# A branch hint at the head of ScalarE's and VectorE's streams, for a taken branch at their end

## The chip, the cores and the metric

The kernel runs on one core of one Trainium2 chip. The metric is device time in microseconds; the time before is the median of four runs, 162.29 us (162.15 to 162.35). The profile is of one further execution, with its own time.

## The reference

```python
def setup_inputs():
    batch, seq, dim = 32, 512, 1024
    return {"x": np.random.randn(batch, seq, dim).astype(np.float32)}

def reference(x):
    relu_x = np.maximum(x, 0)
    return np.mean(relu_x, axis=-1).astype(np.float32)
```

Each of the 16,384 rows of 1,024 float32 numbers is clipped at zero and averaged. The input has 64 MiB, the output 64 KiB.

## The kernel before, in words

The rows are laid over the 128 partitions so that each partition holds 128 neighbouring rows (`J` = 128). A tile is 16 of them for every partition (`NB` = 16): 128 x 16 x 1024 numbers, 8 MiB. There are seven full tiles (`full` = 7) in three buffers, `rows0` to `rows2` (`BUFS` = 3). The eighth tile comes in smaller and smaller pieces so that little work is left behind the last byte: `row_pieces` of 8, 4, 2 and 1 rows, and the last row as `col_pieces` of 512, 256 and 256 columns, in a tile of its own, `last`. All loads and the store are issued by SP, in this order, on one queue. Each load has a semaphore of its own, `loaded[i]`, which counts to 16 when all sixteen transfer engines have landed their share. From the fourth tile on SP waits (`buf_free`) until ScalarE and VectorE have finished the tile that held the buffer.

ScalarE takes the even rows (`act_row`, L15: an activation with Relu and a sum into one column of `sums`), VectorE the odd ones (`dve_row`, L20: a maximum with zero and a sum). In the trace each such row is two instructions, the operation and the read of its accumulator. Both write their elementwise result back over the input. GpSimd scales finished columns of `sums` into `res` (L132, L155). The second-last row is split between ScalarE (448 columns) and VectorE (576). Of the last row, ScalarE takes the first 512 columns, VectorE the next 256, and then VectorE, at L165, takes the last 256 columns and two extra columns in which the partial sums of the other two pieces stand. So L165 ends the last mean. SP waits for it, stores `res` (L173), clears the semaphores (L177) and waits for the store (L178).

The order on every engine is that in which the function writes it: there is no scheduler. The frame around the kernel has three barriers of all engines at the start, one at L195 and two at L55; `issue_ahead_of_entry_barrier` moves the first load on SP ahead of the first of them. A branch from the frame's first block to the kernel's block (L206) stands on every engine between the first barrier and the second. ScalarE's first instruction behind the barriers is a load of its function table, and GpSimd's is the fill of `scale`, which VectorE waits for before its first row.

The program consists of one stream of instructions for each engine. ScalarE's and VectorE's streams are the long ones, with 131 and 132 recorded instructions that count as work; the loops over rows are written out, so neither stream has a loop.

Of the kernel before, what the change touches and what calls it, by code (L numbers as in the profile page):

```python
# [1 line left out]

# [4 lines left out]

F32 = mybir.dt.float32
ALU = mybir.AluOpType
ACT = mybir.ActivationFunctionType  # L10


def act_row(nc, src, acc):

    return nc.scalar.activation(out=src, in_=src, func=ACT.Relu, accum_out=acc)  # L15


def dve_row(nc, src, acc, init=None):

    return nc.vector.tensor_scalar(  # L20
        out=src, in0=src, scalar1=0.0, scalar2=init,
        op0=ALU.max, op1=ALU.add, accum_out=acc,
    )


def issue_ahead_of_entry_barrier(nc):


    entry, body = nc.cur_f.blocks[0].instructions, None
    for block in nc.cur_f.blocks[1:]:  # L30
        for k, ins in enumerate(block.instructions):
            if ins.opcode == "DMACopy":
                body, load = block.instructions, k
                break
        if body is not None:
            break
    first = body[load]
    assert first.engine == mybir.EngineType.SP and not first.sync_info.on_wait
    assert all(i.opcode in ("Drain", "EventSemaphore") or i.engine != first.engine for i in body[:load])
    del body[load]  # L40
    at = next(k for k, i in enumerate(entry) if i.engine == first.engine and i.opcode == "Drain")
    entry.insert(at, first)


@with_exitstack
def kernel(
    ctx: ExitStack,
    tc: tile.TileContext,
    x: bass.AP,
    out: bass.AP,  # L50
):


    tc.close()
    tc.compile()  # L55

    nc = tc.nc
    P = nc.NUM_PARTITIONS
    xf = x.flatten_outer_dims()
    R, D = xf.shape  # L60
    assert R % P == 0
    J = R // P
    inv = 1.0 / D
    xr = xf.rearrange("(p j) d -> p j d", p=P, j=J)
    outr = out.flatten().rearrange("(p j) -> p j", p=P, j=J)

    NB = 16
    BUFS = 3
    full = J // NB - 1

    row_pieces = [8, 4, 2, 1]
    assert sum(row_pieces) == NB - 1
    col_pieces = [512, 256, 256]
    assert sum(col_pieces) == D

    def sbuf(name, *shape):
        return ctx.enter_context(nc.sbuf_tensor(name, list(shape), F32))

    bufs = [sbuf(f"rows{b}", P, NB, D) for b in range(BUFS)]
    sums, res, part = sbuf("sums", P, J), sbuf("res", P, J), sbuf("part", P, 2)  # L80


    last = sbuf("last", P, D + 2)
    scale = sbuf("scale", P, D // 4 + 2)


    loaded = [nc.alloc_semaphore(f"loaded{i}") for i in range(full + len(row_pieces) + len(col_pieces))]
    act, dve, pool = (nc.alloc_semaphore(n) for n in ("act", "dve", "pool"))
    stored = nc.alloc_semaphore("stored")


    def load(i, dst, src):
        nc.sync.dma_start(out=dst, in_=src).then_inc(loaded[i], 16)

    def buf_free(t):

        if t >= BUFS:
            nc.sync.wait_ge(act, t - BUFS + 1)
            nc.sync.wait_ge(dve, t - BUFS + 1)

    for t in range(full):
        buf_free(t)
        load(t, bufs[t % BUFS][:, :, :], xr[:, t * NB:(t + 1) * NB, :])
    j0 = full * NB
    buf_free(full)
    xt = bufs[full % BUFS]
    lo, i = 0, full
    for n in row_pieces:
        load(i, xt[:, lo:lo + n, :], xr[:, j0 + lo:j0 + lo + n, :])
        lo, i = lo + n, i + 1  # L110
    c = 0
    for w in col_pieces:
        load(i, last[:, c:c + w], xr[:, J - 1, c:c + w])
        c, i = c + w, i + 1


    nc.gpsimd.memset(scale[:, :], inv).then_inc(pool, 1)  # L117

    def rows(i, xt, lo, n, j0):
        nc.scalar.wait_ge(loaded[i], 16)  # L120
        nc.vector.wait_ge(loaded[i], 16)
        for k in range(lo, lo + n):
            j = j0 + k
            done = (dve_row if j % 2 else act_row)(nc, xt[:, k, :], sums[:, j:j + 1])
            if k >= lo + n - 2:
                done.then_inc(dve if j % 2 else act, 1)

    def finish(after, lo, hi):

        nc.gpsimd.wait_ge(act, after)  # L130
        nc.gpsimd.wait_ge(dve, after)
        nc.gpsimd.tensor_scalar(  # L132
            out=res[:, lo:hi], in0=sums[:, lo:hi], scalar1=inv, scalar2=0.0, op0=ALU.mult, op1=ALU.add,
        )

    nc.vector.wait_ge(pool, 1)
    for t in range(full):
        rows(t, bufs[t % BUFS], 0, NB, t * NB)
    finish(full, 0, j0)
    lo, i = 0, full  # L140
    for n in row_pieces[:-1]:
        rows(i, xt, lo, n, j0)
        lo, i = lo + n, i + 1
    finish(i, j0, j0 + lo)


    prev = xt[:, NB - 2, :]
    nc.scalar.wait_ge(loaded[i], 16)
    act_row(nc, prev[:, :448], part[:, 0:1]).then_inc(act, 1)
    nc.vector.wait_ge(loaded[i], 16)  # L150
    dve_row(nc, prev[:, 448:], part[:, 1:2]).then_inc(dve, 1)
    n_done = i + 1
    nc.gpsimd.wait_ge(act, n_done)
    nc.gpsimd.wait_ge(dve, n_done)
    nc.gpsimd.tensor_scalar(  # L155
        out=res[:, J - 2:J - 1], in0=part[:, 0:1], scalar1=part[:, 1:2], scalar2=inv, op0=ALU.add, op1=ALU.mult,
    ).then_inc(pool, 1)
    nc.scalar.wait_ge(loaded[i + 1], 16)
    act_row(nc, last[:, :512], last[:, D:D + 1]).then_inc(act, 1)
    nc.vector.wait_ge(loaded[i + 2], 16)  # L160
    dve_row(nc, last[:, 512:768], last[:, D + 1:D + 2]).then_inc(dve, 1)
    nc.vector.wait_ge(act, n_done + 1)
    nc.vector.wait_ge(dve, n_done + 1)
    nc.vector.wait_ge(loaded[i + 3], 16)
    nc.vector.scalar_tensor_tensor(  # L165
        out=last[:, 768:], in0=last[:, 768:], scalar=0.0, in1=scale[:, :], op0=ALU.max, op1=ALU.mult,
        accum_out=res[:, J - 1:J],
    ).then_inc(dve, 1)


    nc.sync.wait_ge(pool, 2)
    nc.sync.wait_ge(dve, n_done + 2)
    nc.sync.dma_start(out=outr, in_=res[:, :]).then_inc(stored, 16)  # L173

    used = [s.num for s in (*loaded, act, dve, pool)]
    assert used == list(range(used[0], used[0] + len(used)))
    nc.sync.sem_clear(range(used[0], used[-1] + 1))  # L177
    nc.sync.wait_ge(stored, 16).then_inc(stored, -16)  # L178

    issue_ahead_of_entry_barrier(nc)  # L180


# [1 line left out]
_INS = ['x']  # L184
_OUTS = [((32, 512), 'float32')]


# [23 lines left out]
```

## Time and profile before

| What | Value |
|---|---|
| Median of four runs | 162.29 us |
| Profiled execution, its own time | 162.34 us |
| Span from its first to its last instruction | 161.0 us |
| Read from HBM | 67.11 MB, 417 GB/s over the span |
| A 128x1024 row on ScalarE, mean of 64 | 1036 ns, and 187 ns for the accumulator |
| A 128x1024 row on VectorE, mean of 64 | 1208 ns, and 83 ns for the accumulator |
| The store, from issue to landing | 1.5 us |
| GpSimd busy | 1.3 us |

Rows of the page's first part give an engine's busy microseconds, the share of the span and the number of instructions. The DMA line cuts the span into 40 slices; a digit is the mean busy share of the sixteen transfer engines in tenths. In the part on queues, a row gives the number of packets, megabytes and the time that the packets took as a share of sixteen engines' span. `q1 hardware_dynamic` is the queue of SP's loads and store; `q14 instruction` carries instructions to the engines. A group of instructions is a line: engine, operation, output and input, shape and count, then the busy time, the mean of one in ns, and the idle time of the engine ahead of them with what ended it. On a timeline each row has the start and the duration in microseconds. Besides these views the trace holds a record of each packet (queue, start, duration, bytes) and the time at which each of the sixteen transfer engines raised a load's semaphore, called a landing here.

### The profile page before, as it was taken

What the parts mean: (1) busy time and instruction counts of PE and PEld (TensorE: products, weight loads), DVE (VectorE), ACT (ScalarE), POOL (GpSimd) and SP (SyncE); (2) the same over time, 40 slices, a digit from 0 to 9 for tenths busy, and PEclk for the clock granted to TensorE, in tenths of its full rate; (3) what the DMA queues carried; (4) which work ended last, traced back from release to release, by engine and by line L of the source; (5) the groups of instructions that cost most, each with busy time, mean ns of one, the idle gap of its engine ahead of it and who ended that gap; (6) DMA issues with size and microseconds to landing.
All of it is one profiled execution on the core that took longest, in us unless ns stands there. A gap on an engine that the chain in (4) does not pass through costs nothing. (4 is left out here: it accounts for less than half of the span.)

```text
span 161.0 us, 336 instructions
## 1 busy us (share of the span) xinstructions
DVE 74.3 (46%) x132; ACT 69.2 (43%) x131; POOL 1.3 (1%) x8
## 2 busy tenths in 40 slices
DVE  0000049800696008940089400992029900498994
ACT  3000049600694008920089200990029800496974
POOL 1000000000000000000000000000000000000001
DMA  7997997997997997998998998998998998999991
GB/s 261 521 456 326 521 456 326 521 456 326 521 456 326 521 440 342 525 407 374 521 407 374 505 423 374 505 423 374 505 423 374 505 423 374 407 448 399 405 392 49
DMA packets 2162, 67.19 MB, mean 417 GB/s; under 512 B 240, under 2 KB 624, under 8 KB 880
## 3 DMA queue, kind: packets, MB, share of 16 engines
q1 hardware_dynamic: 2160, 67.18, 97.2%
q14 instruction: 2, 0.02, 0.0%
HBM read 67.11 MB, written 0.07 MB: 417 GB/s over the span
## 5 line engine op out<-in xcount | busy, mean ns | idle before, releaser
L20 DVE TENSOR_SCALAR_CACHE_REDUCE rows<-rows 128x1024 f32<-128x1024 f32 x64 | 73.3, 1208 | 84.7 <-DMA rows<-in_x_dram 84.6
L15 ACT ACTIVATE rows<-rows 128x1024 f32<-128x1024 f32 x64 | 66.2, 1036 | 88.1 <-DMA rows<-in_x_dram 88.0
L15 ACT ACTIVATION_READ_ACCUMULATOR rows<-rows 128x1 f32 x64 | 12.0, 187 | 0.0
L20 DVE DVE_READ_ACCUMULATOR rows<-rows 128x1 f32 x64 | 5.3, 83 | 0.0
L15 ACT ACT_TABLE_LOAD x1 | 1.3, 1283 | 1.4 <-PEq L55 1.4
L132 POOL TENSOR_SCALAR res<-sums 128x112 f32<-128x112 f32 (+1 forms) x2 | 0.5, 250 | 155.5 <-DVE rows L20 155.5
L15 ACT ACTIVATE last<-last 128x512 f32<-128x512 f32 x1 | 0.6, 630 | 0.0
L20 DVE TENSOR_SCALAR_CACHE_REDUCE last<-last 128x256 f32<-128x256 f32 x1 | 0.4, 420 | 0.2 <-DMA last<-in_x_dram 0.2
L165 DVE SCALAR_TENSOR_TENSOR last<-last,scale 128x258 f32<-128x258 f32 x1 | 0.4, 429 | 0.1
L117 POOL MEMSET scale<- 128x258 f32 x1 | 0.3, 315 | 1.0 <-POOLq L55 1.0
L155 POOL TENSOR_SCALAR res<-part 128x1 f32<-128x1 f32 x1 | 0.3, 264 | 0.6 <-DVE rows L20 0.6
L15 ACT ACTIVATION_READ_ACCUMULATOR last<-last 128x1 f32 x1 | 0.2, 187 | 0.0
L195 POOL MEMSET const-bfloat16-1.0<- 128x1 bf16 x1 | 0.1, 101 | 0.0
L195 POOL MEMSET const-uint8-127<- 128x1 uint8 x1 | 0.1, 101 | 0.0
L195 POOL MEMSET const-float32-0.0<- 128x1 f32 x1 | 0.1, 98 | 0.2 <-issue 0.2
L195 POOL MEMSET const-float32-1.0<- 128x1 f32 x1 | 0.1, 98 | 0.0
L20 DVE DVE_READ_ACCUMULATOR last<-last 128x1 f32 x1 | 0.1, 82 | 0.0
L165 DVE DVE_READ_ACCUMULATOR last<-last,scale 128x1 f32 x1 | 0.1, 82 | 0.0
## 6 DMA issues: line engine op xcount, KB each, us to landing
rows<-in_x_dram SPq DMA_DIRECT2D x1, 4096.0 KB, 39.1
rows<-in_x_dram SPq DMA_DIRECT2D x1, 2048.0 KB, 43.6
rows<-in_x_dram SPq DMA_DIRECT2D x1, 1024.0 KB, 45.6
rows<-in_x_dram SPq DMA_DIRECT2D x1, 512.0 KB, 46.5
last<-in_x_dram SPq DMA_DIRECT2D x1, 256.0 KB, 46.6
last<-in_x_dram SPq DMA_DIRECT2D x2, 128.0 KB, 46.4
rows<-in_x_dram SPq DMA_DIRECT2D x7, 49.2
out_dram<-res SPq DMA_DIRECT2D x1, 64.0 KB, 1.5
```

The source lines that it names most:

```text
L15: return nc.scalar.activation(out=src, in_=src, func=ACT.Relu, accum_out=acc)
L20: return nc.vector.tensor_scalar(out=src, in0=src, scalar1=0.0, scalar2=init, op0=ALU.max, op1=ALU.add, accum_out=acc,)
L117: nc.gpsimd.memset(scale[:, :], inv).then_inc(pool, 1)
L132: nc.gpsimd.tensor_scalar(out=res[:, lo:hi], in0=sums[:, lo:hi], scalar1=inv, scalar2=0.0, op0=ALU.mult, op1=ALU.add,)
L155: nc.gpsimd.tensor_scalar(out=res[:, J - 2:J - 1], in0=part[:, 0:1], scalar1=part[:, 1:2], scalar2=inv, op0=ALU.add, op1=ALU.mult,).then_i ...
L165: nc.vector.scalar_tensor_tensor(out=last[:, 768:], in0=last[:, 768:], scalar=0.0, in1=scale[:, :], op0=ALU.max, op1=ALU.mult, accum_out=r ...
L195: nc = _bacc.Bacc("TRN2", target_bir_lowering=False, num_devices=1)
```

## The change

Behind the allocation of the semaphores, ScalarE and VectorE set a register, `flag`, to zero. All engines then branch to a new block, `rows_begin`, which holds the whole kernel. In it the first instruction of ScalarE and of VectorE is a prefetch hint (`BranchPrefetchHint`, marked "LikelyTaken") for a branch that is their last: it compares `flag` with 1, is always taken, and goes to `rows_end`, an empty block that follows directly. The other three engines get an unconditional branch to `rows_end`. On SP the first load still stands ahead of the first barrier; all later loads stand behind the new branch. The rows, the loads, the waits and the tiles are as before.

```diff
     stored = nc.alloc_semaphore("stored")
+
+
+
+    hinted = (nc.scalar, nc.vector)
+    flag = nc.alloc_registers("flag", engines=[e.engine for e in hinted])
+    nc.regs_mov(flag, 0)
+    nc.br("rows_begin", engines=mybir.ALL_ENGINES)
+    body = ctx.enter_context(nc.body("rows_begin", valid_engines=mybir.ALL_ENGINES))
+    hints = [e.mark_branch_hint_location() for e in hinted]
...
     nc.sync.wait_ge(stored, 16).then_inc(stored, -16)
 
+    for e, hint in zip(hinted, hints):
+        e.br_lt(flag, 1, on_true="rows_end", on_false="rows_begin").branch_hint(hint)
+    nc.br("rows_end", engines=[e for e in mybir.ALL_ENGINES if e not in (h.engine for h in hinted)])
+    nc.switch_bb("rows_end")
+
     issue_ahead_of_entry_barrier(nc)
```

## The prediction

> **What bounds the kernel now.** I read the page's busy table and DMA line first, then the groups, then the transfers in a window round the one odd queue, last the timeline of the end.
>
> ```profile
> DVE 74.3 (46%) x132; ACT 69.2 (43%) x131; POOL 1.3 (1%) x8
> DMA  7997997997997997998998998998998998999991
> q1 hardware_dynamic: 2160, 67.18, 97.2%
> q14 instruction: 2, 0.02, 0.0%
> L20 DVE TENSOR_SCALAR_CACHE_REDUCE rows<-rows 128x1024 f32<-128x1024 f32 x64 | 73.3, 1208 | 84.7 <-DMA rows<-in_x_dram 84.6
> L15 ACT ACTIVATE rows<-rows 128x1024 f32<-128x1024 f32 x64 | 66.2, 1036 | 88.1 <-DMA rows<-in_x_dram 88.0
> ```
>
> Both compute engines are idle more than half the span, and nearly all of that idle time ends when a load lands (84.6 of 84.7 us, 88.0 of 88.1 us). The loads' queue fills 97.2% of sixteen transfer engines. So the end is set by whichever transfer engine finishes its share last, and the compute engines matter only in the last two microseconds. A second queue, q14, moves two packets of instructions. The transfers between 60 and 70 us show them:
>
> ```profile
> q1 hardware_dynamic: 77, 4.39, 102.1%
> q14 instruction: 2, 0.02, 0.4%
> ```
>
> In the stretches 0 to 60 and 66 to 161 us the answer has no q14 row: both packets fall here. The trace's packet records place them: 8,192 bytes each, 309 ns each, starting at 65.04 and 65.13 us, while ScalarE and VectorE both work on the third tile's rows. Sixteen load packets are in flight at any time, one per transfer engine, and each packet starts 4 ns before its predecessor ends, so every engine's chain can be followed. The two fetch packets sit in the chains of two different engines. The load packets right behind them took 2.988 and 2.979 us, where the 64 KB packet's median is 2.418 us. So each fetch delays its engine by 0.305 us for itself (309 less the 4 ns of overlap) and 0.57 us for the slow packet behind it: 0.87 us.
>
> That delay lasts to the end, as each engine has its own fixed share. It can be read from the sixteen landings of each load. In the third load (before the fetches) the last two land at 60.92 and 61.03 us, the third-last at 60.87. In the fourth the last two land at 80.89 and 80.96, the third-last at 80.37. The gap of the last to the third-last was 0.16 us and is 0.59 us from there on: 0.595, 0.594, 0.593, 0.593, 0.594, 0.594, 0.598, and 0.530, 0.523, 0.565 for the three column pieces. So two lagging engines deliver the end of every load.
>
> The end of the run, on the timeline:
>
> ```profile
> 158.05 0.63 ACT L15 ACTIVATE last<-last 128x512 f32<-128x512 f32 x1
> 158.40 0.42 DVE L20 TENSOR_SCALAR_CACHE_REDUCE last<-last 128x256 f32<-128x256 f32 x1 [0.21 <-DMA last<-in_x_dram]
> ...
> 158.58 0.19 ACT L15 ACTIVATION_READ_ACCUMULATOR last<-last 128x1 f32 x1
> 158.74 0.08 DVE L20 DVE_READ_ACCUMULATOR last<-last 128x1 f32 x1
> 158.93 0.43 DVE L165 SCALAR_TENSOR_TENSOR last<-last,scale 128x258 f32<-128x258 f32 x1
> 159.28 0.08 DVE L165 DVE_READ_ACCUMULATOR last<-last,scale 128x1 f32 x1
> 159.43 0.35 SPq L173 DMA_DIRECT2D out_dram<-res  x1
> ```
>
> VectorE's last column piece starts at 158.40 us, 24 ns after its load's last landing (158.376). L165 follows VectorE's own work at 158.93, the store is issued at 159.43, and SP's last wait ends the span at 161.01.
>
> **The change part by part.** *The flag, the branch to rows_begin and the hint (ScalarE, VectorE).* Three sequencer instructions an engine ahead of everything else. A branch between two blocks is already in the old program (L206), and its price can be bounded: ScalarE goes from the release of the first barrier to its next DRAIN in 92 ns with that branch between (0.706 to 0.798 us), and in 91 ns at the second barrier with none (1.034 to 1.125). So about 0 to 1 ns, as if nothing were executed. The register move and the hint are in no row; from below 0, from above VectorE's costliest sequencer record here, the 141 ns wait of L164: at most 0.3 us an engine. Cover: ScalarE's table load ends at 2.72 us and its first row starts at 22.37, VectorE's at 22.48. Some 19 us of waiting hides it; without that cover it would cost at most its 0.3 us.
>
> *The branch to rows_begin on SP, POOL and TensorE.* On SP the second to fourteenth load stand behind it (the first is issued ahead of the barrier, as before). The second is issued at 1.43 us and first needed when the first load runs out at 21.4 us on the earliest engine. On POOL the memset that VectorE's first row waits for stands behind it, done at 1.75 us. TensorE has nothing. Cost 0.
>
> *The branches at the end.* ScalarE's last operation ends at 158.77 and VectorE's at 159.36; SP ends at 161.01. A compare-and-branch between 0 and 141 ns has 1.65 us of cover. SP's own branch to rows_end stands behind its last wait with no cover: 0 to 1 ns by the L206 row, 141 ns by the far bound. I take 0.
>
> *The hint's effect on fetches.* Here the whole time is decided. The fetches at 65 us come from no branch: the old streams run straight on, and each of ScalarE and VectorE (the only two engines with long streams, 131 and 132 recorded instructions) fetches one packet 83 ns apart from the other, in the same row of the same tile. I read this as fetching ahead: at 65 us neither engine stops for it (rows follow at 1.04 and 1.14 us spacing), and nothing is fetched from there to the end, so what they bring is needed near the end or not at all. The new program tells the fetcher of a branch, marked likely taken, whose target is the next instruction. If the fetcher follows the hint, the block to have ready is the target's, which is there already or arrives as before, and the straight-on block is not fetched until the branch is executed, after the last rows.
>
> Then the two engines lose their 0.87 us each, and the third-last engine sets the landings. The end moves by what the tail's first wait gains: VectorE's piece starts 24 ns after the third-last landing of its load, 157.853 in place of 158.376, so at 157.877; it is free, as the split row before it moves up by 0.59 us too. The last piece (158.139 in place of 158.704) is in before it is needed. L165 and the store move by 0.52 us. The sum: -0.52 + 0 + 0 us. On the profiled execution, 162.34 us with its span of 161.0, that is 161.82; on the median of the runs, 162.29, which lies 0.05 below, 161.77. Bounds of this term: -0.60 (the largest gap of landings) if the tail gains more than I see, and -0.22 if the two fetches now fall at 159 to 160 us and one packet of 0.309 us stands ahead of the store's.
>
> The Trainium skill, "Runtime: NRT & Kernel Launch", section "Instruction fetch mechanics", says that prefetch is purely sequential and that a block boundary is mostly hidden. The second half is not so here (0.87 us on each of two engines that end last); by the first half the hint would do nothing and the sum would be 162.29. The same section speaks against the change: a taken branch outside the two-page window stops until its page is fetched. No row here shows such a stop.
>
> **The rivals.**
>
> *The hint does not do it (no effect, or the fetch only moves).* The two packets come at 65 us again, or at about 1.5 us when the hint is executed, by which time all sixteen engines stream (first packets at 1.01 to 2.21 us). Either way each of the two engines carries one fetch, and the end stays: 162.29, with up to 0.14 from SP's branch. For it: nothing in the trace of before shows a hint obeyed, and one dropped fetch of two gains only 0.06 (last against second-last landing). Against: the target lies straight on, so an early copy would make the later fetch needless, and the first packets already take 2.9 to 3.2 us, which may swallow part of a delay.
>
> *The hint adds a fetch.* The target's block is fetched at the hint although it is there, and the straight-on block at 65 us as before. Place: the same two transfer engines. Price: a second 0.87 us on each, so 163.16. It decides as soon as one engine carries two packets. For it: it needs only a fetcher that doesn't look at what it holds. Against: such a fetcher would more likely replace one fetch by the other.
>
> *The end stops for code.* The straight-on block is asked for only at the end's branch, and ScalarE or VectorE stand until it is there. From asking to use I have only the store as a measure: 1.5 us from issue to landing. VectorE's branch could be executed at about 158.8, so its code is there at 160.3, before SP is done at 160.5. It decides when the fetch takes over 1.7 us; at twice the store, 3.1 us, it costs 1.4 us, less the 0.52 gained: 163.2.
>
> **How the numbers follow.** The forecast has 57%: 161.77, by itself 161.69 to 162.07 (the two bounds of its term). No effect or a moved fetch has 28%: 162.2 to 162.45. An added fetch has 8% and a stop at the end 7%. What a measurement of this kernel can tell from no change is about 0.2%, 0.32 us. Faster by more is 57%, within it 28%, slower 15%. The range runs from 161.6 (the -0.60 bound and 0.1 for scatter of runs, which go from 162.15 to 162.35) to 162.45 (no effect with SP's branch at its far bound) and leaves out the two slower cases.
>
> **What would show it.** In the profile after: q14 with no packet between 3 and 157 us; the last landing of each load within 0.2 us of the third-last from the fourth load on; VectorE's last piece near 157.9 and the store near 158.9. Wrong if q14 still shows two packets inside the loads (second case), four (third), or if the store moves up and the time does not (fourth).

## The result and the profile after

| | before | after |
|---|---|---|
| Median | 162.19 us (59 runs, 161.96 to 162.71) | 161.94 us (38 runs, 161.59 to 162.25) |
| Ratio | | 0.9983, 95% interval 0.9978 to 0.9987 |
| Profiled execution | 162.34 us, span 161.0 | 161.98 us, span 160.6 |

The change gains 0.25 us, 0.17% (by the interval 0.13 to 0.22%). The forecast was a gain of 0.52 us. The direction and the cause came as forecast; the size is half.

The page of the kernel after: the busy row, the DMA line, the whole part on queues, and the two costliest groups.

```profile
DVE 74.3 (46%) x132; ACT 69.2 (43%) x131; POOL 1.3 (1%) x8
DMA  7997997997998998998999979979979969899992
q1 hardware_dynamic: 2160, 67.18, 97.5%
L20 DVE TENSOR_SCALAR_CACHE_REDUCE rows<-rows 128x1024 f32<-128x1024 f32 x64 | 73.4, 1209 | 84.3 <-DMA rows<-in_x_dram 84.1
L15 ACT ACTIVATE rows<-rows 128x1024 f32<-128x1024 f32 x64 | 66.2, 1036 | 87.6 <-DMA rows<-in_x_dram 87.4
```

What is missing is the reading: there is no q14 row. No instruction packet starts in the whole span. The compute engines do the same work, and their idle time still ends with landings, 0.4 to 0.6 us less of it.

The new instructions, from the answers for the three lines that they have (operation, count, duration in ns as lowest, median and highest, first and last start in us):

```profile
L95 ACTq MOVE  x1: 35/35/35, 1.4 to 1.4; - x1
L95 DVEq MOVE  x1: 44/44/44, 1.5 to 1.5; - x1
...
L98 ACTq BRANCH_PREFETCH_HINT  x1: 40/40/40, 1.5 to 1.5; - x1
L98 DVEq BRANCH_PREFETCH_HINT  x1: 51/51/51, 1.5 to 1.5; - x1
...
L190 ACTq COMPARE_BRANCH  x1: 53/53/53, 157.7 to 157.7; - x1
L190 DVEq COMPARE_BRANCH  x1: 60/60/60, 158.6 to 158.6; - x1
```

All lie under cover. No unconditional branch is recorded. The end of the timeline of the kernel after:

```profile
158.03 0.42 DVE L20 TENSOR_SCALAR_CACHE_REDUCE last<-last 128x256 f32<-128x256 f32 x1 [0.29 <-DMA last<-in_x_dram]
...
158.55 0.43 DVE L174 SCALAR_TENSOR_TENSOR last<-last,scale 128x258 f32<-128x258 f32 x1
158.90 0.09 DVE L174 DVE_READ_ACCUMULATOR last<-last,scale 128x1 f32 x1
159.06 0.35 SPq L182 DMA_DIRECT2D out_dram<-res  x1
```

VectorE's last column piece starts at 158.03 us (before: 158.40), L174 at 158.55 (158.93), the store at 159.06 (159.43). All three move by 0.37 to 0.38 us, and the span by 0.37. The landings of the trace go with it: the load of VectorE's piece lands last at 158.004 us, before at 158.376. From the fourth load on the last landing is 0.17 to 0.21 us behind the third-last, where it was 0.52 to 0.60. What lies outside the span hardly changed: 1.33 us before, 1.35 after.

### The profile page after: what moved, and what is told of

Read it like the earlier page. It is cut to its first block, busy times and chain, and to the rows that moved or that the text cites. A ratio compares the mean times of both kernels' runs of the same rounds, so it can differ in the third digit from the quotient of the medians.

```text
span 160.6 us, 342 instructions
## 1 busy us (share of the span) xinstructions
DVE 74.3 (46%) x132; ACT 69.2 (43%) x131; POOL 1.3 (1%) x8
## 5 line engine op out<-in xcount | busy, mean ns | idle before, releaser
L174 DVE SCALAR_TENSOR_TENSOR last<-last,scale 128x258 f32<-128x258 f32 x1 | 0.4, 429 | 0.1
L174 DVE DVE_READ_ACCUMULATOR last<-last,scale 128x1 f32 x1 | 0.1, 85 | 0.0
```

Of the source, the lines that this page charges most:

```text
L174: nc.vector.scalar_tensor_tensor(out=last[:, 768:], in0=last[:, 768:], scalar=0.0, in1=scale[:, :], op0=ALU.max, op1=ALU.mult, accum_out=r ...
```

## The experiments

Theory A: the hint keeps the two instruction fetches out of the load stream, and the rest of the change costs nothing. Theory B: the 0.52 us were there, and branches and register move ate half. Theory C: the blocks and branches bring the gain. Theory D: the gain is what the two fetching transfer engines stick out over the other fourteen, which differs from one execution to the next.

**No hint.** The changed kernel without its hints:

```diff
-    hints = [e.mark_branch_hint_location() for e in hinted]
...
-    for e, hint in zip(hinted, hints):
-        e.br_lt(flag, 1, on_true="rows_end", on_false="rows_begin").branch_hint(hint)
+    for e in hinted:
+        e.br_lt(flag, 1, on_true="rows_end", on_false="rows_begin")
```

> The blocks, the flag, the compare-and-branch at the end, but no hint. Theory A (the hint keeps the two instruction fetches out of the load stream, and the rest of the change costs nothing): two packets on q14 near 65 us again, the last landing of the fourth to tenth load 0.3 to 0.6 us behind the third-last, time as before, 162.19 us, ratio 0.999 to 1.001. Theory B (the forecast gain of 0.52 us was there, and branches and register move ate half of it): slower than before by about 0.25 us, 162.45. Theory C (the gain comes from the blocks and branches, not the hint): 161.94, no packet on q14 within the loads.

162.25 us against 162.24 before, ratio 1.0003 (0.9992 to 1.0013). The transfers of this kernel between 60 and 70 us show the fetches back, at 64.93 and 65.04 us by the packet records:

```profile
q1 hardware_dynamic: 78, 4.39, 102.2%
q14 instruction: 2, 0.02, 0.4%
```

From the fourth load on the last landing is 0.48 to 0.54 us behind the third-last. So C falls, and B with it: blocks, flag, move and branches together cost nothing that the interval can show (at most 0.21 us).

**The changed kernel again.** No edit.

> The changed kernel once more, on the same chip as the others of this group. Theory A: 161.94 us, 0.25 us under before, no packet on q14 within the loads; the last landing 0.1 to 0.3 us behind the third-last in every load. If the size of the gain depends on the order in which the sixteen transfer engines happen to run (theory D), this execution's last landing will differ from the first one's (158.29 us) by 0.1 us or more, though nothing was changed.

161.97 us, ratio 0.9983 (0.9974 to 0.9992). No q14 row; the last landing of all loads at 158.23 us against 158.29 in the first profile, 0.15 to 0.20 us behind the third-last from the fourth load on. The gain repeats. The difference of 0.06 us is below the 0.1 that I named for D, so this pair doesn't speak for D; the twelve executions below do.

**One engine hints.** The hint for ScalarE alone, then for VectorE alone (the same edit with `nc.vector`):

```diff
-    hints = [e.mark_branch_hint_location() for e in hinted]
+    hint = nc.scalar.mark_branch_hint_location()
...
-    for e, hint in zip(hinted, hints):
-        e.br_lt(flag, 1, on_true="rows_end", on_false="rows_begin").branch_hint(hint)
+    for e in hinted:
+        branch = e.br_lt(flag, 1, on_true="rows_end", on_false="rows_begin")
+        if e is nc.scalar:
+            branch.branch_hint(hint)
```

> Only ScalarE hints; VectorE has its branch without a hint. Theory A: one packet on q14 near 65 us (VectorE's), one transfer engine late. As the end waits for the last of sixteen, one late engine costs nearly as much as two: 162.05 to 162.19 us, a gain of 0 to 0.15. If the two fetches cost independently: half of the gain, 162.07. If one engine fetches both packets: two or none on q14.

> Only VectorE hints. Theory A: one packet on q14 near 65 us (ScalarE's), 162.05 to 162.19 us, like the ScalarE-only kernel within 0.1 us. A difference of more than 0.15 us between the two would say that the two transfer engines that fetch do not stick out equally.

ScalarE alone: 162.17 us, ratio 0.9997 (0.9986 to 1.0008). VectorE alone: 162.11 us, ratio 0.9990 (0.9981 to 0.9999). The page's part on queues with ScalarE's hint alone:

```profile
q1 hardware_dynamic: 2160, 67.18, 97.4%
q14 instruction: 1, 0.01, 0.0%
```

One packet, at 67.23 us. The part with VectorE's hint alone:

```profile
q1 hardware_dynamic: 2160, 67.18, 97.3%
q14 instruction: 1, 0.01, 0.0%
```

Here the one packet stands at 65.20 us. So each hint takes away one of the two. That it is the fetch of its own engine, and the one left the other's, is the plain reading but not shown: a packet's record doesn't name the engine that it is for. The times lie 0.07 and 0.13 us under 162.24; by their intervals they can't be told from half of the gain, nor from each other, and the second (down to 0.9981) not from the whole gain of 0.9983. In both profiles the one late transfer engine doesn't set the end (table below).

**The hint late.** Both engines hint directly ahead of the branch, at the end of their rows:

```diff
-    hints = [e.mark_branch_hint_location() for e in hinted]
...
+    hints = [e.mark_branch_hint_location() for e in hinted]
     for e, hint in zip(hinted, hints):
```

> Both engines hint directly ahead of the branch, behind the last rows, in place of at the head. Theory A, with the hint acting only on fetches that come after it: the two packets at 65 us are back, time as before, 162.19 us. If the hint acted when the program is loaded, or the branch alone did: 161.94 and no packets.

162.21 us, ratio 1.0002 (0.9993 to 1.0011), two packets at 67.36 and 67.37 us. So the hint acts while the program runs, and only on fetches after it; that the hinted branch is in the program does nothing. This run has a surprise: two fetches, and the last landing only 0.11 to 0.15 us behind the third-last.

**128 empty instructions: no experiment, but two repeats.** Both the kernel before and the changed one got this, to raise the number of fetches:

```diff
         rows(t, bufs[t % BUFS], 0, NB, t * NB)
+        if t == 0:
+            for e in (nc.scalar, nc.vector):
+                for _ in range(128):
+                    e.nop(nofuse=True)
```

> The kernel before, with 128 empty instructions on ScalarE and on VectorE behind the first tile's rows, in an idle time of 10 us. It adds instructions and no work. Theory A (one fetch of 8,192 bytes, 128 instructions of 64, for each 128 instructions passed): four packets on q14 within the loads, two for each engine's stream, on the same two transfer engines, the last landing 1.2 to 1.5 us behind the third-last, time up by 0.87 us, 163.05. If a fetch costs only its own 0.31 us: 162.5. If fetches do not set the end: 162.19.

> The changed kernel with the same 128 empty instructions: the hinted branch now lies one block of 128 further on. If the hint makes the target's block the one to have ready at once: a packet for each engine near 1.5 us, none at the later boundary, and the time of before, 162.2. If it only holds back the straight-on fetch in the block of the branch: a packet for each engine at the first boundary (20 to 65 us), none at the second, 162.2 too. If the hint loses its effect: four packets, 163.05. If nothing is fetched ahead at all, an engine stops in the middle of its rows for its code, and the stop shows as a gap between rows that no landing ends.

The empty instructions leave no trace: there are 336 recorded instructions without the hint, as before, and 342 with it, as after, and no fetch more. So I take these for the two kernels once more: 162.20 us, ratio 1.0000 (0.9991 to 1.0009), with packets at 64.96 and 67.26 us; and 161.86 us, ratio 0.9979 (0.9970 to 0.9989), with no q14 row. They say nothing on the cost of more fetches. The second repeat shows something else: from the fourth load on its last landing is 0.25 to 0.34 us behind the third-last, though nothing is fetched. With the late hint it is 0.11 to 0.15 with two fetches. So that gap, which I had named as a sign, doesn't tell by itself whether there was a fetch; the q14 row does.

**The kernel before again**, for a second profile.

> The kernel before once more, for a second profile of it. Theory A: two packets on q14 near 65 us, two slow load packets of about 2.98 us behind them. Theory D: the gap of last to third-last landing differs from 0.59 us by 0.1 or more, since it depends on where the two transfer engines stand among the sixteen.

162.39 us, span 161.1; packets at 65.17 and 67.58 us, the load packets behind them 2.69 and 2.98 us. The last landing is 0.41 to 0.47 us behind the third-last: over 0.1 away from 0.59, as D has it.

**128 real instructions.** 256 waits that are already reached, two in an instruction:

```diff
         rows(t, bufs[t % BUFS], 0, NB, t * NB)
+        if t == 0:
+            for _ in range(256):
+                nc.scalar.wait_ge(loaded[0], 16)
+                nc.vector.wait_ge(loaded[0], 16)
```

> The kernel before, with 256 waits for the first load's semaphore, already reached, on ScalarE and on VectorE behind the first tile's rows: 128 instructions more on each engine, two waits in each, in an idle time of 10 us. (The 128 empty instructions of the earlier kernels are not in the built program, so those two were repeats.) Theory A with one fetch of 8,192 bytes for each 128 instructions passed: four packets on q14 within the loads, two near 31 to 35 us and two near 65 to 68 us, on the same two transfer engines, each 0.6 to 0.9 us late for each. Theory D (the end moves by what the two engines stick out over the other fourteen, which was 0.04 to 0.51 us with one fetch each): they now stick out by 0.9 to 1.4 us, so 0.6 to 0.9 us over before: 162.8 to 163.1. If the fetches do not set the end: 162.2.

163.09 us, ratio 1.0051 (1.0037 to 1.0065): 0.81 us over 162.28. The page's part on queues:

```profile
q1 hardware_dynamic: 2160, 67.18, 96.8%
q14 instruction: 4, 0.03, 0.0%
```

The packets start at 30.96, 33.42, 65.40 and 68.14 us, and the last landing is 1.20 to 1.28 us behind the third-last. The end of its timeline:

```profile
159.11 0.42 DVE L20 TENSOR_SCALAR_CACHE_REDUCE last<-last 128x256 f32<-128x256 f32 x1 [0.24 <-DMA last<-in_x_dram]
...
160.14 0.35 SPq L177 DMA_DIRECT2D out_dram<-res  x1
```

The store comes 0.71 us later than in the first profile of before (159.43), behind a column piece that waits 0.24 us for its load. The waits themselves are hidden: VectorE's first row of the second tile still waits for its load, 10.50 us of idle time. So 16 KB more of instructions, 0.02% of what the kernel moves, cost 0.5% of its time.

**The same with the hint.**

> The changed kernel with the same 128 instructions more on ScalarE and VectorE; the hinted branch now lies one block of 128 further on than the block that follows the hint. If the hint makes the target's block the next one to have ready, at once: a packet for each engine near 1.5 us and none later; one fetch on each engine, so the time of before, 162.1 to 162.3. If it only holds back the straight-on fetch in the branch's own block: a packet for each engine at 31 to 35 us and none at 65: 162.1 to 162.3 too. If both fetches are held back until they are needed, an engine stands still in the middle of its rows for its code: a gap between two rows that no landing ends. If the hint has no effect at this distance: four packets and the time of the kernel with the waits alone.

162.25 us, ratio 0.9998 (0.9989 to 1.0007), 0.84 us under the kernel with the waits alone. The transfers of this kernel from 30 to 36 us:

```profile
q1 hardware_dynamic: 38, 2.49, 96.7%
q14 instruction: 2, 0.02, 0.6%
```

From 60 to 70 us the answer has one row alone:

```profile
q1 hardware_dynamic: 82, 4.46, 102.9%
```

The first pair comes (30.88 and 33.44 us), the second doesn't. Nothing is fetched at 1.5 us, where the hint stands. So the hint neither calls for its target at once nor stops all fetching ahead: it holds back the last of the straight-on fetches. That this is the one that would come as the engine enters the block of the hinted branch fits, but no record shows where one block ends and the next begins.

**Twelve executions, engine by engine.** The chains of packets (each starts 4 ns before its predecessor ends) give, for each transfer engine, when its last 64 KB packet ended. Taking away a fetch (its own time less 4 ns, and what the packet behind it took over 2,418 ns) gives the same engine's end without it; the latest of the sixteen then tells what the fetches cost in that execution. This is an estimate: it takes it that the other engines would have run as they did. With the 128 waits alone each of the two engines carries two fetches, and their delays are added up. All times in us:

```
kernel               fetch delays   latest   without   cost
before                0.87  0.87    138.55   138.04    0.51
no hint               0.85  0.85    138.44   138.02    0.42
before again          0.57  0.86    138.58   138.18    0.41
empty instr., before  0.85  0.56    138.36   138.02    0.34
hint late             0.84  0.86    138.37   138.33    0.04
128 waits, hint       0.57  0.83    138.40   138.40    0
ScalarE hints         0.84          138.27   138.27    0
VectorE hints         0.56          138.34   138.34    0
after                               138.25
after again                         138.13
empty instr., after                 138.31
128 waits             1.27  1.84    139.26   138.12    1.14
```

With two fetches the cost goes from nothing to 0.51, 0.28 on average over the six. The fetching engines don't end last by themselves: without their fetch they would end 0.36 to 1.0 us before the latest. This headroom differs from one execution to the next; as much of a fetch's 0.56 to 0.87 us as it covers is free, and the rest moves the end. With one fetch the headroom was 0.92 and 0.59 us, more than the delay, and the cost zero. So it was with two fetches in the kernel with waits and hint, whose latest engine in this execution is one without a fetch (the kernel's median of 162.25 us is that of before); six of its load packets took 2.63 to 3.07 us at 41 us, where nothing was fetched. Without any estimate, the latest ends average 138.45 us in the six executions with two fetches and 138.23 in the three with none: 0.22 us.

## Why the prediction was right, and where it was off

- *What bounds the kernel*: right. A kernel that differs by two instruction packets differs in time; one with two more is 0.81 us slower.
- *The price of a fetch, 0.87 us on its engine*: right as the upper end. In the executions with one or two fetches it is 0.56 to 0.87 us, and the packet behind takes 2.67 to 2.99 us. Its own share is 0.31 to 0.34 us. Of the four in the kernel with the waits one reaches 0.98 us, with 3.08 us for the packet behind it.
- *The new instructions at nothing*: right. The bound of 0 to 141 ns holds them all: 35 to 60 ns each. ScalarE's table load starts 0.13 us later (1.57 us) under 19 us of cover. SP's end branch, for which I kept 0.14 us, shows 0.02 at most in what lies outside the span.
- *The hint holds the straight-on fetch back until the branch*: right as far as it goes. It doesn't come at 65 us. That it comes behind the branch isn't seen: no packet starts up to the end of the span, so my bound for a packet ahead of the store's did not come into play.
- *The term of -0.52 us*: mis-sized. The step that failed is "the third-last engine sets the landings", with 157.853 us for VectorE's wait. It is true of the one execution that I had, where it can be worked out, and I took it for the kernel's cost. That execution, 162.34 us, is 0.15 us over the median of 59 runs, and its two fetching engines stuck out furthest of the six with two fetches: 0.51 us, where the six average 0.28 and go down to nothing. The spans of the six average 160.92 us, of the three with none 160.64: 0.28 us. The medians give 0.25 us here, 0.27 and 0.38 in the two repeats. My range for this case, 161.69 to 162.07, holds the result, but for another reason than the one I gave for its upper end. That the forecast time of 161.77 us is only 0.17 off is in part luck: the gain was put 0.27 us too high, but it was taken off 162.29, the median of four runs, which lies 0.10 over that of 59.
- *The chances*: I had put what can be told from no change at 0.32 us and given 57% to a larger gain. The gain is smaller than that, so by my own line the result lies in the part that I gave 28%, though not for the reason that stood there: the hint does act, and 59 and 38 runs tell 0.25 us from none.
- *The rivals*: "no effect" is what happens without the hint or with a late one. "An added fetch" didn't come from the hint; its mechanism is the kernel with 128 waits, where two more fetches cost 0.81 us against the 0.87 that I named. "The end stops for code" isn't seen: 1.33 us outside the span with two fetches, 1.35 without.
- *The rule of the Trainium skill* ("Runtime: NRT & Kernel Launch", "Instruction fetch mechanics") that prefetch is purely sequential fits the two packets at 65 us without a hint, and not the one packet or none there with one or two hints. That crossing a boundary is mostly hidden fits the engine that fetches (the rows go on at 1.04 and 1.14 us spacing) and not the transfer engine that carries the packet (0.56 to 0.98 us late). The stop at a taken branch, of which the same section speaks, doesn't show: the branches at the end take 53 and 60 ns.

What stays open: the size is known as 0.2 to 0.4 us and no closer, by six profiles against three and by the medians. Why the two fetching engines had between 0.36 and 1.0 us of headroom is not known. The share of one engine's hint is not settled, as the intervals of the two kernels overlap.

## What to carry to other kernels

Where the transfer engines are full to the end, a small packet on one of them can cost more than its own time: look at which engine ends last, and what it carried besides the loads. A lag read from one execution is the gain of that execution; where a maximum over sixteen engines sets the end, ask how far each would stand from the latest without the lag, and take several profiles before giving it a size. In this kernel a hint ahead of a block of instructions kept what follows it from being fetched in the middle of the loads.

## What the runs showed that was not expected

- A fetch costs its transfer engine 0.56 to 0.98 us for 309 to 345 ns of its own: the load packet behind it takes 2.67 to 3.08 us in place of 2.418.
- The streams are fetched in packets of 8,192 bytes, and 128 more instructions on an engine bring one more packet, which fits 64 bytes an instruction.
- In some executions three to eight load packets at a time take 2.6 to 3.1 us with no fetch near them (at 11.5 us in the kernel where ScalarE alone hints, at 50 us with VectorE alone, at 35 and 40 us in before again, at 26 and 41 us in the kernel with waits and hint). What slows them is not known; they are part of why the headroom differs.
